# Norm squares added by accumulating DMA and VectorE, 1/rms inside the first product, memory scaled in the mixer's output stage

## The chip, the cores and the metric

The kernel runs on one core of a Trainium2 chip. The metric is the device time of one execution in microseconds (us). A "product" below is one matrix product of 24 matmuls into one PSUM bank.

## The reference

Two layers of a streaming-encoder block on 512 tokens of width 1024 (float32), and a final RMS norm:

```python
for l in range(2):
    x = x + 0.5 * swiglu(rmsnorm(x, ffn1_norm[l]), w1, w3, w2)          # hidden width 2816
    proj = rmsnorm(x, mix_norm[l]) @ w_in[l]                            # q, f, i, g | u
    o_a = hgrn2_mixer(q_a, f_a, i_a, g_a, ...)                          # gated linear recurrence, 4 heads
    o_b = multiscale_pool(u_b, pool_w[l], pool_scale[l])
    x = x + concatenate([o_a, o_b]) @ w_out[l]
    x = x + mem_cross_attention(rmsnorm(x, xa_norm[l]), rmsnorm(mem, mem_norm[l]), wq, wkv, wo)
    x = x + 0.5 * swiglu(rmsnorm(x, ffn2_norm[l]), w1, w3, w2)
return rmsnorm(x, final_norm)
# rmsnorm(x, g) = x * rsqrt(mean(x*x) + 1e-6) * g
```

## The kernel before

x is held transposed in SBUF (`xT`, eight tiles of 128 channels by 512 tokens). A float32 product is made of three float32r matmuls (`mm3`, lines 84 to 86): each operand is split into a rounded high part and a rest (`split`: ScalarE rounds, line 76 or 79; VectorE subtracts, line 77 or 80). Weights are split too, on the chip, after their load.

**Norms.** A `Norm` splits x times its gain as soon as a tile of x is final (`part`, giving `h`). 1/rms depends on the token alone, so it is multiplied in behind the product. `square` squares each tile on ScalarE, and GpSimd adds the eight squares one after another (line 388). `tick` is called behind each of the first products that use the norm: at tick `late` (2; 3 for the very first norm) the channels are summed by matmuls with ones and 1/rms is made (`col_rsqrt`), and a diagonal matrix of it (`diagonals`, eight small VectorE instructions); one tick later, that is behind the next product, a matmul spreads it to a row (`col_to_row`, ScalarE copies it as `rrow`). Only then can the first products be scaled and leave PSUM.

**FFN** (`ffn`). The hidden width is cut into 22 columns j in three parts. Columns 0 to 5 are plain: a product with w1, one with w3. The others go in pairs through `Pairs.block`, which makes seven half-size products in place of eight and needs the scaled right operands `b11` to `t4`. These are made by the generator `operands` in 14 steps, four in each column from j = 2. `project` multiplies by w2 in two halves and adds to x; in the second half it calls `after`, which is the next norm's `add`: for x tiles 0 to 3 behind its first two groups, for 4 to 7 behind each one's last matmul.

**Mixer, attention.** `mix` ends with `project` (groups of 24 matmuls, and after each an entry of `between`). `xattn` begins by loading `memT` in four pieces (`mt`), scaling them by 1/rms of the memory (line 914) and splitting them with the gain (`mn`); its first products, the keys, take `mn`. Its norm needs no row, and its 1/rms is not wanted before the scores.

**Weights** (`Weights`). `next` splits the next plain weights `SPLIT` = 3 ahead and loads up to `LOAD` = 7 ahead. Weights, split parts, `h`, operands and most other tiles share 38 slots of 4 KB.

**Order.** Each engine's queue is in the order of a scheduler that runs at build time: the program's order is its priority, and an instruction that its own time estimate finds not ready is passed over for a later one. On the chip the order is fixed.

Of the kernel before, what the change touches and what calls it, by code (L numbers as in the profile page):

```python
# [30 lines left out]

PLAIN = 6
PARTS = ((0, 8), (8, 16), (16, 22))
# [13 lines left out]
def trunk_kernel(ctx: ExitStack, tc: tile.TileContext, ap: dict, out: bass.AP):  # L47
# [41 lines left out]
    class Weights:  # L89

        SPLIT, LOAD = 3, 7

# [128 lines left out]
    for l in range(L):  # L223
        for w1, w3, w2 in (("ffn1_w1", "ffn1_w3", "ffn1_w2"), ("ffn2_w1", "ffn2_w3", "ffn2_w2")):
            for lo, hi in PARTS:
                for j in range(lo, hi):
                    if j < PLAIN:
                        wts.cols(ap[w1][l], j)
                        wts.cols(ap[w3][l], j)
                    elif j % 2 == 0:  # L230
                        wts.block(ap[w1][l], j)
                        wts.block(ap[w3][l], j)
                if hi == NJ and w1 == "ffn2_w1" and l == L - 1:
                    for k in [*range(lo, hi)] * 2:
                        wts.rows(ap[w2][l], k, 1, 0, D)
                else:
                    wts.project(ap[w2][l][lo * P:hi * P, :], hi - lo)
            if w1 == "ffn1_w1":
                for c in (4, 5, 6, 7, 0, 1, 2, 3, 12, 13, 14, 15):
# [12 lines left out]
                wts.project(ap["xa_wo"][l], NK)  # L252
# [87 lines left out]
    def diagonals(col, n=NT):  # L340

        dg = s_tile([P, 2, NT, P], F32R, "dg")
        hi = sm.tile([P, NT], F32R, tag="chi", name="chi")[:, :n]
        lo = sm.tile([P, NT], F32, tag="clo", name="clo")[:, :n]
        dve.tensor_copy(hi, col)
        dve.tensor_tensor(lo, col, hi.bitcast(F32), op=ALU.subtract)
# [12 lines left out]
    class Norm:  # L359
# [3 lines left out]

        def __init__(self, gain, l, row=True, late=2):
            self.gain, self.l, self.row, self.late = gain, l, row, late
            self.h = [None] * NK
            self.sq = None
            self.ticks = 0
            self.waiting = []
            self.r = self.col = None  # L370
# [250 lines left out]

    def ffn(norm, after, start=None, between=None):
        pairs = None
        for lo, hi in PARTS:
            a = []
            for j in range(lo, hi):
                if j >= PLAIN:
                    ahl = s_tile([P, 2, T], F32R, "ahl")
# [21 lines left out]
                norm.then(left)  # L650
                if j == 2:
                    pairs = Pairs(norm)
                    operands = pairs.operands()
                if j > 1:
                    next(operands, None)
                    next(operands, None)
                if p3 is None:
                    p3 = ps_tile()
                    col_matmul(p3, norm.h)
                norm.tick()  # L660
                t3 = tp.tile([P, T], F32, tag="up", name="t3", bufs=3)
# [8 lines left out]
                if between:  # L670
                    next(between, None)
                if j > 1:
                    next(operands, None)
                    next(operands, None)
            for _ in operands:
# [6 lines left out]

    def mix(l, norm, after):
        f = [s_tile([P, 2, T], F32, "f") for _ in range(2)]
# [6 lines left out]
        for h in range(H):  # L691
            ps = ps_tile()
            col_matmul(ps, norm.h)
            norm.tick()

# [18 lines left out]
        def products(a, b):  # L714

            t = tp.tile([P, T], F32, tag="sq", name="qk")
            hl = s_tile([P, 2, T], F32R, "qkp")
# [159 lines left out]
        def read(h):  # L877
# [4 lines left out]
            for i in range(NT):  # L882
# [3 lines left out]
                pe.matmul(ps[:, i * P:(i + 1) * P], vs[i], d0[:, i], start=False, stop=i == NT - 1)  # L886
            sq[h] = tp.tile([P, T], F32, tag="sq", name="osq")
            act.activation(sq[h], ps, AF.Square)
# [6 lines left out]
        def emit(h):  # L895
# [12 lines left out]
    def xattn(l, norm, after):  # L908

        mn = []  # L910
        for k2 in range(NK // 2):
            mt = s_tile([P, 2, M], F32, "mt")
            nc.sync.dma_start(mt, ap["memT"][:, 2 * k2:2 * k2 + 2])
            dve.tensor_tensor(mt, mt, memr.rearrange("p (o m) -> p o m", o=1).broadcast_to([P, 2, M]), op=ALU.mult)
            t = s_tile([P, 2, 2, M], F32R, "mn")
            for e in range(2):
                k = 2 * k2 + e
                split(t[:, 0, e], t[:, 1, e], mt[:, e], scale=vcol("mem_norm", l, k))
                mn.append((t[:, 0, e], t[:, 1, e]))
        kT = []  # L920
        for c in range(NK):
# [82 lines left out]
    def finish(a):  # L1004
# [12 lines left out]
        for half in range(2):  # L1017
# [4 lines left out]
            for js in [[j] for j in range(n - 2)] + tail:  # L1022
                for j in js:
                    w[j] = wts.next()
                for i in mine:
                    sl = slice(i * P, (i + 1) * P)
                    final = half and i == mine[1]
                    for hf in range(2):
# [7 lines left out]
                        dve.scalar_tensor_tensor(yi, accs[i, hf], 0.5, yi, op0=ALU.mult, op1=ALU.add)  # L1036
                        sq = tp.tile([P, 512], F32, tag="sq", name="fsq")
                        act.activation(sq, yi, AF.Square, accum_out=ss[:, i, hf:hf + 1])
# [20 lines left out]

    norm = Norm("ffn1_norm", 0, late=3)  # L1060
    wts.first()
    for d in range(NK):
        norm.part(d)
    for d in range(NK):
        norm.square(d)

    def begin(norm):
# [3 lines left out]
        for p, k2 in ((0, 0), (0, 1), (1, 0), (1, 1), (0, 2), (1, 2), (0, 3), (1, 3),  # L1071
# [16 lines left out]
    for l in range(L):  # L1088
        nxt = Norm("mix_norm", l)
        if l == 0:  # L1090
            ffn(norm, nxt.add, start=begin, between=early())
        else:
            ffn(norm, nxt.add)
        norm, nxt = nxt, Norm("xa_norm", l, row=False)
        mix(l, norm, nxt.add)
        norm, nxt = nxt, Norm("ffn2_norm", l)
        xattn(l, norm, nxt.add)
        norm = nxt
        if l + 1 < L:
            nxt = Norm("ffn1_norm", l + 1)  # L1100
            ffn(norm, nxt.add)
            norm = nxt
        else:
            finish(ffn(norm, None))

# [48 lines left out]
```

## Time and profile before

| | us |
|---|---|
| median of 3 runs (2178.58 to 2180.31) | 2178.6 |
| the profiled execution's own time | 2181.06 |
| its span, first to last instruction | 2179.3 |
| TensorE (PE) busy in the span | 2135.4 |
| VectorE (DVE) busy | 1403.0 |
| ScalarE (ACT) busy | 886.7 |
| GpSimd (POOL) busy | 289.8 |

The span is what the trace covers; the execution's own time has 1.8 us around it. PE busy 2135.4 of 2179.3 us leaves 43.9 us in which no matmul ran, 7.35 us of it ahead of the first one and 8.2 us behind the last. Where a matmul ran at a lower granted clock, it counts as busy all the same.

### The profile page before, as it was taken

Reading aid. Unit: us, or ns where it says so; the run is one execution under the profiler, and the core shown is the slowest. Engines: PE = TensorE matmul, PEld = TensorE weight load, DVE = VectorE, ACT = ScalarE, POOL = GpSimd, SP = SyncE. Lnnn points to the kernel's source line nnn. Section 1 sums busy time; section 2 is a strip of 40 time slices with the busy share of each in tenths; the row PEclk is TensorE's granted clock in tenths of the full one; section 3 lists DMA queues with packets and bytes.
Section 4 is the critical chain, followed back from the end, with each engine's and each line's share of the span. In section 5 each row is a group of like instructions: output and inputs, shape, how many; then the busy total and the mean of one; then the engine's idle time right before and its main releaser. Section 6 shows DMA issues by size and latency. Waiting matters only on the chain.

```text
span 2179.3 us, 31306 instructions
## 1 busy us (share of the span) xinstructions
PE 2135.4 (98%) x12470; PEld 1886.3 (87%) x12470; DVE 1403.0 (64%) x2212; ACT 886.7 (41%) x1372; POOL 289.8 (13%) x249
## 2 busy tenths in 40 slices
PE   7999999999999999999999999999999999999998
PEld 5789898788788888999988998988888888889896
DVE  5857566687736575756567575668775565757565
ACT  4535344312436243434444353453044443435254
POOL 2200002302200220000020000024211002100002
PEclk9999999999999999999999999999999999999999
DMA  5375453212323235645424646422023322465543
GB/s 204 93 191 138 141 147 135 67 59 87 107 97 122 78 90 157 172 134 155 144 72 120 175 130 179 150 83 87 31 97 116 116 89 75 117 181 138 162 126 110
DMA packets 103746, 265.55 MB, mean 122 GB/s; under 512 B 9904, under 2 KB 9904, under 8 KB 103600
## 3 DMA queue, kind: packets, MB, share of 16 engines
q1 hardware_dynamic: 93520, 228.37, 31.6%
q0 software_dynamic: 9216, 33.56, 9.0%
q8 instruction: 98, 1.61, 0.3%
q10 hardware_dynamic: 864, 1.63, 0.2%
q14 instruction: 48, 0.39, 0.1%
HBM read 261.42 MB, written 2.10 MB: 121 GB/s over the span
## 4 chain that ended last, share of the span: by engine, by line
PE 90%; DVE 5%; ACT 2%; issue 1%; POOL 1%; DMA 0%; SPq 0%; POOLq 0%; ACTq 0%; DVEq 0%
PE ps L86 17%; PE ps L84 17%; PE ps L85 17%; PE acc L84 11%; PE acc L85 11%; PE acc L86 11%; PE ps L765 2%; DVE wlo L77 1%; ACT whi L76 1%; DVE h L80 1%; PE ps L885 0%; POOL t L666 0%; DVE bsum L496 0%; DVE qkp L77 0%; PE ps L886 0%
## 5 line engine op out<-in xcount | busy, mean ns | idle before, releaser
L77 DVE TENSOR_TENSOR wlo<-raw,whi 128x1024 fp32r<-128x1024 f32 (+1 forms) x327 | 406.3, 1265 | 72.7 <-issue 44.8
L76 ACT CAST whi<-raw 128x1024 fp32r<-128x1024 f32 (+1 forms) x327 | 331.2, 1046 | 168.4 <-PE acc L86 65.9
L84 PE MATMUL ps<-h,whi 128*128 128x512 f32 x824 | 322.9, 393 | 8.8 <-ACT h L79 7.4
L85 PE MATMUL ps<-h,whi 128*128 128x512 f32 x824 | 321.5, 391 | 2.2 <-DVE h L80 2.2
L86 PE MATMUL ps<-h,wlo 128*128 128x512 f32 x824 | 321.0, 391 | 2.6 <-DVE wlo L77 2.6
L84 PE MATMUL acc<-bh,whi 128*128 128x256 f32 x768 | 218.2, 285 | 4.5 <-ACT whi L76 3.8
L84 PE MATMUL ps<-bh,whi 128*128 128x256 f32 x768 | 217.6, 284 | 1.2 <-ACT whi L76 1.2
L86 PE MATMUL ps<-bh,wlo 128*128 128x256 f32 x768 | 217.7, 284 | 0.5 <-DVE wlo L77 0.5
L85 PE MATMUL ps<-bl,whi 128*128 128x256 f32 x768 | 217.5, 283 | 0.0
L85 PE MATMUL acc<-bl,whi 128*128 128x256 f32 x768 | 217.4, 283 | 0.0
L86 PE MATMUL acc<-bh,wlo 128*128 128x256 f32 x768 | 217.1, 284 | 0.0
L77 DVE TENSOR_TENSOR wlo<-wsum,whi 128x1024 fp32r<-128x1024 f32 x128 | 156.6, 1224 | 77.1 <-ACT whi L76 42.0
L84 PEld LDWEIGHTS ps<-h,whi 128*128 128x128 f32 x824 | 155.2, 188 | 41.8 <-ACT h L79 7.4
L76 ACT CAST whi<-wsum 128x1024 fp32r<-128x1024 f32 x128 | 134.2, 1049 | 133.2 <-DVE wsum L164 106.2
L85 PEld LDWEIGHTS ps<-h,whi 128*128 128x128 f32 x824 | 155.2, 188 | 36.8 <-DVE h L80 5.4
L86 PEld LDWEIGHTS ps<-h,wlo 128*128 128x128 f32 x824 | 155.1, 188 | 36.7 <-DVE wlo L77 4.3
L134 POOL DMA_DIRECT2D wsum<-in_ffn_w_dram x64 | 55.6, 869 | 777.8 <-PE ps L86 260.2
L84 PEld LDWEIGHTS acc<-bh,whi 128*128 128x128 f32 x768 | 147.7, 192 | 6.6 <-ACT whi L76 4.9
L84 PEld LDWEIGHTS ps<-bh,whi 128*128 128x128 f32 x768 | 147.3, 192 | 2.5 <-ACT whi L76 1.8
L86 PEld LDWEIGHTS ps<-bh,wlo 128*128 128x128 f32 x768 | 147.6, 192 | 0.7 <-DVE wlo L77 0.7
L85 PEld LDWEIGHTS acc<-bl,whi 128*128 128x128 f32 x768 | 147.8, 192 | 0.5
L85 PEld LDWEIGHTS ps<-bl,whi 128*128 128x128 f32 x768 | 147.6, 192 | 0.6
(255 smaller groups left out, 4513.9 us busy)
## 6 DMA issues: line engine op xcount, KB each, us to landing
raw<-in_ffn_w_dram SPq DMA_DIRECT2D x205, 512.0 KB, 4.0
wsum<-in_ffn_w_dram SPq DMA_DIRECT2D x128, 256.0 KB, 3.1
wsum<-in_ffn_w_dram POOLq DMA_DIRECT2D x64, 512.0 KB, 5.6
raw<-in_ffn_w_dram SPq DMA_DIRECT2D x66, 256.0 KB, 4.9
raw<-in_w_in_dram SPq DMA_DIRECT2D x32, 512.0 KB, 3.3
raw<-in_w_out_dram SPq DMA_DIRECT2D x16, 512.0 KB, 3.4
raw<-in_xa_wk_dram SPq DMA_DIRECT2D x16, 512.0 KB, 3.3
raw<-in_xa_wq_dram SPq DMA_DIRECT2D x16, 512.0 KB, 3.3
```

The source lines that it names most:

```text
L76: act.copy(hi, src)
L77: dve.tensor_tensor(lo, src, hi.bitcast(F32), op=ALU.subtract)
L80: dve.scalar_tensor_tensor(lo, src, scale, hi.bitcast(F32), op0=ALU.mult, op1=ALU.subtract)
L84: pe.matmul(o, a[0], b[0], start=start, stop=False, skip_group_check=more)
L85: pe.matmul(o, a[0], b[1], start=False, stop=False, skip_group_check=more)
L86: pe.matmul(o, a[1], b[0], start=False, stop=stop, skip_group_check=more)
L134: nc.gpsimd.dma_start(s1, c2, accum_op=ALU.add)
L765: pe.matmul(o, kg[g][:, hh, sl], rhs, start=True, stop=True)
```

## The change

- `square`: of eight squares, the first goes to a tile `far`, the next three are added to it by accumulating DMAs from GpSimd's queue, and VectorE adds the other four and `far` (four additions). The very first norm has `far=0`: VectorE adds all (seven), and its squares are issued between the first products instead of ahead of them.
- `tick` is called four times within a product (`col_matmul`) in place of once behind it: 1/rms is made behind the fourth of eight k steps of the first product, and its row is made at that product's end (`rest` = 2). Attention's keys still call it once in three products.
- `operands` start as soon as the row is there, from j = 0, two steps behind each product. `diagonals` takes two wide instructions in place of eight small ones.
- Plain weights are split five ahead in place of three; the rules for blocks and for the end of the list stay.
- `memory` (loads, scaling and splitting of `mn`) is a generator of eight steps that the mixer's last `project` advances after its third to eighth group; two steps come behind it.
- PLAIN becomes a tuple of four sixes: no column changes its kind.

```diff
-        SPLIT, LOAD = 3, 7
+        SPLIT, LOAD = 5, 7
...
-            ahead = [*self.ahead(i, self.SPLIT + block)]
-            if i + self.SPLIT == len(self.src) - 1:
-                ahead.append(i + self.SPLIT)
+            ahead = [*self.ahead(i, 4 if block else self.SPLIT)]
+            if i + 3 == len(self.src) - 1:
+                ahead.append(i + 3)
...
     def diagonals(col, n=NT):
...
-        for i in range(n):
-            dve.tensor_scalar(dg[:, 0, i], ident, hi[:, i:i + 1].bitcast(F32), None, op0=ALU.mult)
-            dve.tensor_scalar(dg[:, 1, i], ident, lo[:, i:i + 1], None, op0=ALU.mult)
+        eye = ident.rearrange("p (o t) -> p o t", o=1).broadcast_to([P, n, P])
+        for c in range(2):
+            on = hl[:, c, :n].bitcast(F32).rearrange("p (n o) -> p n o", o=1).broadcast_to([P, n, P])
+            dve.tensor_tensor(dg[:, c, :n], eye, on, op=ALU.mult)
...
         def square(self, d):
-            s = tp.tile([P, T], F32, tag="sq", name="sq")
+            if self.n == 0 < self.FAR:
+                self.far = s = s_tile([P, T], F32, "far")
+            else:
+                s = tp.tile([P, T], F32, tag="sq", name="sq", bufs=4)
             act.activation(s, xT[d], AF.Square)
-            if self.sq is None:
+            if 0 < self.n < self.FAR:
+                nc.gpsimd.dma_start(self.far, s, accum_op=ALU.add)
+            elif self.n == self.FAR:
                 self.sq = s
-            else:
-                a = tp.tile([P, T], F32, tag="sqa", name="sqa")
-                pool.tensor_tensor(a, self.sq, s, op=ALU.add)
-                self.sq = a
+            elif self.n > self.FAR:
+                dve.tensor_tensor(self.sq, self.sq, s, op=ALU.add)
+                if self.far is not None and self.n == self.FAR + 1:
+                    dve.tensor_tensor(self.sq, self.sq, self.far, op=ALU.add)
+            self.n += 1
...
-            if self.ticks == self.late + 1 and self.row:
+            if self.ticks == self.late + self.rest and self.row:
...
-    def col_matmul(ps, parts, n=T):
+    def col_matmul(ps, parts, n=T, tick=None):
         whl = wts.next()
         for k in range(NK):
             mm3(ps[:, :n], (whl[0][:, k, :], whl[1][:, k, :]), parts[k], start=k == 0, stop=k == NK - 1)
+            if tick and k % 2:
+                tick()
...
+        def steps(n=-(-14 // (2 * plain - 2))):
+            nonlocal pairs, operands
+            if norm.r is None:
+                return
+            if pairs is None:
+                pairs = Pairs(norm)
+                operands = pairs.operands()
+            for _ in range(n):
+                next(operands, None)
...
-                    col_matmul(p1, norm.h)
-                norm.tick()
+                    col_matmul(p1, norm.h, tick=norm.tick)
...
-                if j == 2:
-                    pairs = Pairs(norm)
-                    operands = pairs.operands()
-                if j > 1:
-                    next(operands, None)
-                    next(operands, None)
+                steps()
...
         project(NK, parts, 1.0, after, order=MIX_OUT, tiles=(acc_tile, acc_tile),
-                between=[lambda: (scale(3), emit(2)), lambda: emit(3)])
+                between=[lambda: (scale(3), emit(2)), lambda: emit(3), *[lambda: next(mem, None)] * 8])
...
+    def memory(l, mn):
         for k2 in range(NK // 2):
             mt = s_tile([P, 2, M], F32, "mt")
             nc.sync.dma_start(mt, ap["memT"][:, 2 * k2:2 * k2 + 2])
+            yield
             dve.tensor_tensor(mt, mt, memr..., op=ALU.mult)
...
+            yield
...
-    norm = Norm("ffn1_norm", 0, late=3)
+    norm = Norm("ffn1_norm", 0, late=1, rest=1, far=0)
     wts.first()
     for d in range(NK):
         norm.part(d)
-    for d in range(NK):
-        norm.square(d)
...
     def begin(norm):
...
+            if norm.n < NK and p + k2 > 1:
+                norm.square(norm.n)
+            if p > 1 and k2 == 3:
+                norm.tick()
```

## Rows read from the trace of the kernel before

**Rows 1.** Page, busy us of an engine, its share of the span, its instructions.
```profile
PE 2135.4 (98%) x12470; PEld 1886.3 (87%) x12470; DVE 1403.0 (64%) x2212; ACT 886.7 (41%) x1372; POOL 289.8 (13%) x249
```

**Rows 2.** Waits of PE over the span: us in total, times, longest.
```profile
PE acc L333 <- POOL sqa L388: 9.8, 2, 4.9
PE ps L84 <- ACT h L79: 7.4, 1, 7.4
PE acc L84 <- ACT whi L76: 5.6, 6, 1.7
PE ps L86 <- DVE wlo L77: 3.9, 7, 1.0
PE ps L725 <- DVE atd L752: 2.6, 2, 1.3
PE ps L85 <- DVE h L80: 2.2, 3, 0.7
PE ps L84 <- DVE t L648: 1.4, 1, 1.4
```

**Rows 3.** Stretches: length, busy us (count) of PE, PEld, DVE, ACT, POOL; clock, DMA.
```profile
7.35:21.35 14.00, 10.75 (x29) 6.29 (x30) 13.21 (x12) 12.55 (x20) 11.15 (x7) 1.00 1.02 409
30.00:40.00 10.00, 10.00 (x49) 8.37 (x48) 1.01 (x7) 0.00 (x0) 1.03 (x1) 1.00 0.18 59
...
47.00:101.00 54.00, 49.77 (x242) 41.10 (x241) 47.10 (x64) 28.31 (x43) 13.38 (x9) 0.97 0.31 85
...
555.00:571.00 16.00, 16.00 (x72) 13.24 (x71) 9.96 (x9) 5.92 (x9) 4.79 (x3) 1.00 0.40 122
574.50:592.00 17.50, 12.22 (x73) 11.41 (x72) 14.04 (x22) 9.38 (x17) 6.64 (x5) 0.80 0.24 80
810.00:822.00 12.00, 10.81 (x87) 10.36 (x86) 10.80 (x16) 6.98 (x11) 1.59 (x1) 1.00 0.60 201
```

**Rows 4.** Timeline at layer 0's attention: start, us, engine, line, out<-in, idle before.
```profile
573.21 6.77 POOL L388 TENSOR_TENSOR sqa<-sqa,sq 128x512 f32<-128x512 f32 x4 [10.46 <-ACT sq L383]
...
578.78 1.75 DVE L914 TENSOR_TENSOR mt<-mt,memr 128x512 f32<-128x512 f32 x1
...
580.03 1.87 PE L333 MATMUL acc<-ones,sqa 128*128 128x1 f32 x8 [4.89 <-POOL sqa L388]
```

**Rows 5.** Groups of instructions: busy us, mean ns of one, idle before.
```profile
L388 POOL TENSOR_TENSOR sqa<-sqa,sq 128x512 f32<-128x512 f32 x48 | 80.5, 1677 | 83.5 <-ACT sq L383 80.7
...
L164 DVE TENSOR_TENSOR wsum<-wsum,raw 128x512 f32<-128x512 f32 x64 | 43.9, 685 | 0.7
```

**Rows 6.** Line 80: ns min/median/max of its instructions.
```profile
L80 DVE SCALAR_TENSOR_TENSOR h<-xall,vec,h x64: 737/1090/1795, 7.3 to 1815.0; 128x512 fp32r<-128x512 f32 x64
L80 DVE SCALAR_TENSOR_TENSOR mn<-mt,vec,mn x16: 477/482/485, 581.2 to 1658.0; 128x256 fp32r<-128x256 f32 x16
```

**Rows 7.** Line 134, accumulating DMAs of 512 KB: issue in ns, landing in us.
```profile
L134 POOL DMA_DIRECT2D wsum<-in_ffn_w_dram x64: 853/862/1037, 57.4 to 2086.8; - x64
...
DMA to landing us min/median/max: 5.2/5.6/10.3
```

**Rows 8.** Line 913, plain DMAs of 256 KB.
```profile
DMA to landing us min/median/max: 2.5/2.8/2.9
```

**Rows 9.** Timeline at ffn2 of layer 0: 1/rms, its row, the first operand.
```profile
754.94 0.16 DVE L335 TENSOR_SCALAR v<-acc 128x4 f32<-128x4 f32 x1 [4.54 <-PE acc L333]
...
757.89 0.28 DVE L349 TENSOR_SCALAR dg<-fixed,clo 128x128 fp32r<-128x128 f32 x1
...
763.06 0.59 ACT L400 COPY rrow<-acc 128x512 f32<-128x512 f32 x1 [14.73 <-PE acc L356]
...
771.97 0.74 DVE L472 SCALAR_TENSOR_TENSOR top<-xall,vec,rrow 128x512 f32<-128x512 f32 x1
```

**Rows 10.** Timeline at the end of ffn1, layer 0: the second and sixth square.
```profile
357.06 0.62 ACT L383 ACTIVATE sq<-xall 128x512 f32<-128x512 f32 x1
...
371.65 0.62 ACT L383 ACTIVATE sq<-xall 128x512 f32<-128x512 f32 x1
```

More of the change, by code (lines that the diff above doesn't have):

```diff
@@ L29 @@
 SLOTS = 38
-PLAIN = 6
+PLAIN = (6,6,6,6)
 PARTS = ((0, 8), (8, 16), (16, 22))
@@ L226, in trunk_kernel @@
                 for j in range(lo, hi):
-                    if j < PLAIN:
+                    if j < PLAIN[2 * l + (w1 == "ffn2_w1")]:
                         wts.cols(ap[w1][l], j)
@@ L342, in diagonals @@
         dg = s_tile([P, 2, NT, P], F32R, "dg")
[L343 to L346, printed above, removed]
-        for i in range(n):
-            dve.tensor_scalar(dg[:, 0, i], ident, hi[:, i:i + 1].bitcast(F32), None, op0=ALU.mult)
-            dve.tensor_scalar(dg[:, 1, i], ident, lo[:, i:i + 1], None, op0=ALU.mult)
+        hl = sm.tile([P, 2, NT], F32R, tag="chl", name="chl")
+        dve.tensor_copy(hl[:, 0, :n], col)
+        dve.tensor_tensor(hl[:, 1, :n], col, hl[:, 0, :n].bitcast(F32), op=ALU.subtract)
+        eye = ident.rearrange("p (o t) -> p o t", o=1).broadcast_to([P, n, P])
+        for c in range(2):
+            on = hl[:, c, :n].bitcast(F32).rearrange("p (n o) -> p n o", o=1).broadcast_to([P, n, P])
+            dve.tensor_tensor(dg[:, c, :n], eye, on, op=ALU.mult)
         return dg
@@ L359, in trunk_kernel, with __init__ @@
     class Norm:
-        def __init__(self, gain, l, row=True, late=2):
-            self.gain, self.l, self.row, self.late = gain, l, row, late
+        def __init__(self, gain, l, row=True, late=2, rest=2, far=4):
+            self.gain, self.l, self.row, self.late, self.rest, self.FAR = gain, l, row, late, rest, far
             self.h = [None] * NK
-            self.sq = None
+            self.sq = self.far = None
+            self.n = 0
             self.ticks = 0
@@ L619, in done, with ffn @@
             split(self.a[1][0], self.a[1][1], self.t[1])
-    def ffn(norm, after, start=None, between=None):
-        pairs = None
+    def ffn(norm, plain, after, start=None, between=None):
+        pairs = operands = None
+        def steps(n=-(-14 // (2 * plain - 2))):
[7 more added lines that the diff above has]
+                next(operands, None)
         for lo, hi in PARTS:
@@ L626, in ffn @@
             for j in range(lo, hi):
-                if j >= PLAIN:
+                if j >= plain:
                     ahl = s_tile([P, 2, T], F32R, "ahl")
@@ L650, in ffn @@
                 norm.then(left)
-                if j == 2:
-                    pairs = Pairs(norm)
-                    operands = pairs.operands()
-                if j > 1:
-                    next(operands, None)
-                    next(operands, None)
+                steps()
                 if p3 is None:
                     p3 = ps_tile()
-                    col_matmul(p3, norm.h)
-                norm.tick()
+                    col_matmul(p3, norm.h, tick=norm.tick)
                 t3 = tp.tile([P, T], F32, tag="up", name="t3", bufs=3)
@@ L671, in ffn @@
                     next(between, None)
-                if j > 1:
-                    next(operands, None)
-                    next(operands, None)
+                steps()
             for _ in operands:
@@ L680, in ffn, with mix @@
             project(hi - lo, a, 0.5, after if hi == NJ else (lambda d: None), tiles=(acc_tile, ps_tile))
-    def mix(l, norm, after):
+    def mix(l, norm, mem, after):
         f = [s_tile([P, 2, T], F32, "f") for _ in range(2)]
@@ L692, in mix @@
             ps = ps_tile()
-            col_matmul(ps, norm.h)
-            norm.tick()
+            col_matmul(ps, norm.h, tick=norm.tick)
             def forget(h=h, ps=ps):
@@ L714, in products @@
         def products(a, b):
-            t = tp.tile([P, T], F32, tag="sq", name="qk")
+            t = tp.tile([P, T], F32, tag="sq", name="qk", bufs=4)
             hl = s_tile([P, 2, T], F32R, "qkp")
@@ L886, in read @@
                 pe.matmul(ps[:, i * P:(i + 1) * P], vs[i], d0[:, i], start=False, stop=i == NT - 1)
-            sq[h] = tp.tile([P, T], F32, tag="sq", name="osq")
+            sq[h] = tp.tile([P, T], F32, tag="sq", name="osq", bufs=4)
             act.activation(sq[h], ps, AF.Square)
@@ L919, in xattn @@
                 mn.append((t[:, 0, e], t[:, 1, e]))
+            yield
+    def xattn(l, norm, mn, after):
         kT = []
@@ L1036, in finish @@
                         dve.scalar_tensor_tensor(yi, accs[i, hf], 0.5, yi, op0=ALU.mult, op1=ALU.add)
-                        sq = tp.tile([P, 512], F32, tag="sq", name="fsq")
+                        sq = tp.tile([P, 512], F32, tag="sq", name="fsq", bufs=4)
                         act.activation(sq, yi, AF.Square, accum_out=ss[:, i, hf:hf + 1])
@@ L1090, in trunk_kernel @@
         if l == 0:
-            ffn(norm, nxt.add, start=begin, between=early())
+            ffn(norm, PLAIN[0], nxt.add, start=begin, between=early())
         else:
-            ffn(norm, nxt.add)
+            ffn(norm, PLAIN[2], nxt.add)
         norm, nxt = nxt, Norm("xa_norm", l, row=False)
-        mix(l, norm, nxt.add)
+        mn = []
+        mem = memory(l, mn)
+        mix(l, norm, mem, nxt.add)
+        for _ in mem:
+            pass
         norm, nxt = nxt, Norm("ffn2_norm", l)
-        xattn(l, norm, nxt.add)
+        xattn(l, norm, mn, nxt.add)
         norm = nxt
@@ L1100, in trunk_kernel @@
             nxt = Norm("ffn1_norm", l + 1)
-            ffn(norm, nxt.add)
+            ffn(norm, PLAIN[1], nxt.add)
             norm = nxt
         else:
-            finish(ffn(norm, None))
+            finish(ffn(norm, PLAIN[3], None))
 def _layout(inputs):
```

2 lines of the change are left out of this document (removed).

## The prediction

> **What bounds the kernel now.** First the page's table of engines: TensorE is busy 2135.4 us of the 2179.3 us span [rows 1], so no other engine sets the time as a whole. The change takes no matmul away (PLAIN stays at six), so it can win only what TensorE idles, 43.9 us, and what a low clock costs; of the idle time 7.4 us are the wait for the first tile of x and some 8 us follow the last matmul, and neither is touched. Second, TensorE's list of waits [rows 2]: it names what is late. Third, windows around those waits [rows 3], which give the place: length less busy time is idle time, and the clock column shows where the matmuls that did run were slow. The reader should see five places:
> - the head, 7.35 to 21.35: 14.00 less 10.75, 3.25 us idle;
> - the wait for a PSUM bank that the row of 1/rms frees: 1.4 us, once (`t`, line 648);
> - the first FFN, 47 to 101: 4.23 us idle, and a mean clock of 0.97, which over 54 us is 1.6 us more; VectorE is busy 47.1 of the 54 us;
> - the start of attention, 574.5 to 592: 5.28 us idle and a clock of 0.80, up to 3.5 us more, so 8.8 us; the wait for `sqa` stands twice, so layer 1 has it too: 17.6 us;
> - the first block of the three later FFNs: 1.19 us each, 3.6 us; and the mixer's first level (`atd`), 1.3 us in each layer, 2.6 us [rows 2].
>
> All together 34.3 us, which is the most that the parts below can bring.
>
> **Attention's start.** TensorE runs dry after the mixer's product and waits 4.89 us until GpSimd has added the last squares (573.21 plus 6.77 is 579.98) [rows 4]. That addition is not what it needs: the keys take `mn`, and line 914 starts on the first piece of `mt` only at 578.78, behind the additions to x and the splits of `h`. The scheduler put the 1/rms matmuls into the hole. So the late work is the memory's. The change moves, per layer, four loads on SP's queue, four scalings on VectorE (1.75 us for the one shown, beside GpSimd), eight rounded parts on ScalarE and eight of 0.48 us on VectorE [rows 4, 6] into the output stage: at most 11 us of VectorE. In 16 us of that stage VectorE was busy 9.96 [rows 3], so 6 us are free in this stretch alone, which is three of the stage's eight groups (72 of 8 x 24 matmuls): hidden. The loads of 256 KB land in 2.8 us [rows 8] and are short of a group's 5.3 us. If that cover were gone, TensorE would wait as today. The last of four pieces has its scaling behind the end of the stage, so products start with six of eight k steps; I let each layer keep 1.8 us. Gain 2 x 7.0 = 14.0 us (bounds 2 x 5.3, the idle time alone without the two later pieces' wait growing, and 17.6).
>
> **Squares off GpSimd.** Removed: 56 GpSimd additions of about 1.68 us [rows 5]. Added: 35 VectorE additions (four for seven norms, seven for the first) at 0.69 us, the price of line 164, which also adds two float32 tiles in SBUF: 24 us; and 21 accumulating DMAs, 0.86 us of GpSimd each [rows 5, 7]. VectorE gets as much back: `h` took 1.09 us in the median and 1.80 at worst, but 0.74 at best [rows 6]; 64 of them at 0.35 us less are 22 us. So VectorE's total stays, and at a norm's end the four splits (about 1.4 us less together) pay for half of the four additions. In the head the same effect counts at once: three waits for `h` [rows 2] fall into a time when GpSimd adds for 11.15 of 14 us [rows 3], and the squares no longer stand between the `h` pieces on ScalarE. Gain 2.5 us of 3.25 (bounds 0, if the loads of x set the pace, and 3.25).
>
> **The accumulating DMAs' delay.** The trace has none within SBUF. From below, a plain 256 KB load lands in 2.8 us [rows 8]; from above, an accumulating one of 512 KB in 5.6 us in the median, 10.3 at worst [rows 7]. I take 4, between them for half the bytes. The three wait for each other. At the end of ffn1 the second square is done at 357.7 and the sixth, with which `far` is added, at 372.3 [rows 10]; `far` is complete at 369.7, or at 374.5 with 5.6 us each. So at 4 us it costs nothing, at 5.6 us VectorE waits about 2 us, still ahead of the matmuls on h[6]. SP's queue is not touched; GpSimd's holds nothing else there.
>
> One page speaks against this part. The issue of such a DMA took 0.85 to 1.04 us in all 64 cases, on a VectorE that is busy 64% of the time [rows 1, 7]. The Trainium skill, "SBUF — State Buffer", section "SBUF: two separate sides", warns that GpSimd cannot write descriptors while VectorE holds the shared port pair, so that such a DMA waits for the VectorE instruction. By that rule each of the 21 would be late by up to one VectorE instruction; by the row none was. What remains of it is in the third rival.
>
> **1/rms within the first product.** At ffn2 of layer 0 the column sums end at 754.94, the diagonals at 758.17, but the row is copied only at 763.06 and the first operand begins at 771.97 [rows 9]: 3.2 us are work, the rest is the program's order. After the change the row comes about two products (11 us) earlier, and the operands by 15 us or so. In the first FFN that moves VectorE work into a stretch where VectorE does 1.01 of 10 us [rows 3], and the 1.4 us wait for the bank goes. Of the 5.8 us in 47 to 101 I take 4.5 (bounds 2 and 5.8); of the later blocks' 3.6 I take 2.7, since operands no longer share VectorE and ScalarE with the first block's splits there (10.80 of 12 us busy) (bounds 0 and 3.6); of the mixer's 2.6 half, 1.3 (bounds 0 and 2.6). Splitting five ahead gives the plain products more margin in the same stretches and takes four more slots of 38; I count it into these terms. The new diagonals cost two instructions at 0.69 for eight that overlap within 1.7 us: nothing.
>
> The price: at the 1/rms matmuls TensorE now stands close behind the last square. In rows 4 the sums were complete 4.8 us after the last matmul of the stage; with VectorE's additions about 3.5. The fourth k step is done after 12 matmuls of 0.22 us, 2.7 us: 0.8 us too early. The row is planned for the product's end (6.4 us with the sums' own 0.95), and can be there after 3.5 + 0.95 + 3.2 + 0.3, 8.0: 1.6 us too early. The scheduler passes such matmuls over where its own estimate sees the delay, so each of six norms costs between 0 and 2.4 us. I take 0.7, as the waits of rows 2 that come from such near dependences average 0.6 to 0.9 (`wlo`, `whi`): 4.2 us.
>
> **Sum.** 14.0 + 2.5 + 1.4 + 4.5 + 2.7 + 1.3 = 26.4, less 4.2: 22 us. The profiled execution would go from 2181.1 to 2159 us; it lies 2.5 us above the median of the runs, so against 2178.6 I forecast **2156 us**.
>
> **Rivals.**
> - The norms' waits come at their full 2.4 us: six norms, 14.4 us instead of 4.2. For it: the order is fixed from estimates that did not see 20 us of waits in the trace before. Against it: other matmuls of the next product are ready. 2178.6 - 26.4 + 14.4 = 2167 us.
> - The memory's work does not come early: the build-time order may keep it behind the splits of `h`, as it did with loads that lay ready [rows 4]. Against it: the program now names it earlier. Without the 14.0 us: 2170 us. Both of these together give 2181, no change.
> - Slower: `far` is late. If the accumulations land in 10.3 us, as the slowest of 64 did, `far` is complete at 388.6, and VectorE, which works in order, holds the splits h[6] and h[7] behind it; TensorE has use for h[6] some 4 us into the product, so it stands about 12 us at each of the three norms behind an FFN, and about 5 us at the two behind attention, where the squares begin earlier: 46 us, 2178.6 - 22 + 46 = 2203 us. It decides from about 6 us per accumulation. Against it: half the bytes, and no HBM.
>
> **Chances.** The forecast 0.62 (own range 2144, all 34.3 us with no new wait, to 2165); the norms' waits 0.14; no early memory 0.09; both, 0.05; `far` late, 0.10. The range 2143 to 2173 leaves out the last two and little else. About 0.2% (4 us) is what a measurement of this kernel can tell from no change. Faster 0.85, same 0.05, slower 0.10.
>
> **What would show it.** In the profile after: no wait of 4.9 us and no lower clock at attention's start, with the first `mt` scaling ahead of the last additions to x; no line of GpSimd for `sqa`, and `h` at 0.75 us; the row of 1/rms some 9 us after a product begins; operands complete by j = 3 and no wait for `whi` at the first block. Wrong would make it: waits of TensorE at lines of the column sums or the diagonal's product, VectorE waiting for the DMA into `far`, or loads on SP's queue held back for slots at j = 2 to 4, where operands, `h` and deeper splits are held together.

## The result, and the profile after

The changed kernel takes 2151.8 us (median of 4 runs, 2149.14 to 2153.5), the kernel before 2179.5 beside it: a ratio of 0.9872, with an interval from 0.9855 to 0.9889. Forecast were 2156 us. In the profiled executions the span went from 2179.3 to 2147.4 us. TensorE idles 24.2 us of it, where it was 43.9, so 19.7 of the 31.9 us are idle time; the other 12.2 us are less busy time for the same matmuls. The mean granted clock went from 0.994 to 0.997, which is worth about 6.6 us of them (0.006 of 2179.3 less 0.003 of 2147.4, an estimate); what shortened the rest was not isolated.

The table of engines on the page of the kernel after (busy us, share, instructions) answers to [rows 1]:

```profile
PE 2123.2 (99%) x12470; PEld 1880.7 (88%) x12470; DVE 1381.4 (64%) x2161; ACT 885.3 (41%) x1372; POOL 226.5 (11%) x214
```

Its list of what TensorE waited for (us in total, times, longest; the five largest of nine) answers to [rows 2]:

```profile
PE ps L84 <- ACT h L79: 7.2, 1, 7.2
PE ps L86 <- DVE wlo L77: 2.5, 2, 2.1
PE acc L84 <- ACT whi L76: 1.7, 1, 1.7
PE ps L85 <- DVE h L80: 1.2, 2, 0.9
PE ps L84 <- DVE t L668: 0.9, 1, 0.9
```

The wait for `sqa` (9.8 us) is gone, and so are the mixer's for `atd` (2.6 us) and the ones for `whi` at the first blocks: the one that is left stands at the very end. No line of the column sums or of the row's product stands in the list. One wait is new, 2.1 us for a weight's rest (`wlo`).

Stretches of the kernel after (length, busy us and count of PE, PEld, DVE, ACT, POOL, clock, DMA share, GB/s): the head, the first FFN, the last part of the mixer's output stage, and attention's start. They answer to the windows of [rows 3].

```profile
7.20:21.20 14.00, 12.39 (x42) 8.41 (x43) 13.40 (x20) 14.00 (x22) 0.00 (x0) 1.00 1.03 407
...
42.00:96.00 54.00, 51.65 (x265) 43.99 (x264) 44.90 (x63) 27.78 (x42) 16.73 (x9) 0.97 0.38 114
542.00:567.20 25.20, 25.20 (x113) 20.87 (x112) 17.20 (x25) 13.06 (x21) 2.64 (x3) 1.00 0.52 136
567.20:584.00 16.80, 16.80 (x142) 16.76 (x141) 13.40 (x24) 10.27 (x18) 1.94 (x1) 1.00 0.50 161
```

Attention's start was 5.28 us idle at a mean clock of 0.80; now it is never idle, at full clock, and the same holds in layer 1. The first FFN is not better by much: 2.35 us idle where 4.23 were, and the clock of 0.97 is there again.

Why attention starts at once is in VectorE's timeline of the kernel after (start, us, line, out<-in):

```profile
542.97 0.68 DVE L925 TENSOR_TENSOR mt<-mt,memr 128x512 f32<-128x512 f32 x1
...
550.08 0.68 DVE L925 TENSOR_TENSOR mt<-mt,memr 128x512 f32<-128x512 f32 x1
...
556.25 0.68 DVE L925 TENSOR_TENSOR mt<-mt,memr 128x512 f32<-128x512 f32 x1
...
571.58 0.69 DVE L925 TENSOR_TENSOR mt<-mt,memr 128x512 f32<-128x512 f32 x1
```

and in TensorE's, the last matmul of the stage and the first of the keys:

```profile
567.12 0.39 PE L86 MATMUL acc<-h,wlo 128*128 128x512 f32 x1
567.35 0.28 PE L84 MATMUL ps<-mn,whi 128*128 128x256 f32 x1
```

Three of the four pieces of the memory are scaled inside the stage; the fourth comes 4.2 us after the keys' first matmul and still in time. In [rows 4] the first of them came at 578.78, when TensorE had already run dry.

The norm at ffn2 of layer 0, which answers to [rows 9], in the timeline of the kernel after, from the stage's first matmul:

```profile
726.27 0.39 PE L84 MATMUL ps<-h,whi 128*128 128x512 f32 x1
...
731.25 0.68 DVE L394 TENSOR_TENSOR sq<-sq 128x512 f32<-128x512 f32 x1
...
736.47 0.95 PE L333 MATMUL acc<-ones,sq 128*128 128x1 f32 x8
...
737.46 0.16 DVE L335 TENSOR_SCALAR v<-acc 128x4 f32<-128x4 f32 x1 [5.53 <-PE acc L333]
739.06 1.28 DVE L349 TENSOR_TENSOR dg<-fixed,chl 128x512 fp32r<-128x512 f32 x2
...
745.13 0.59 ACT L408 COPY rrow<-acc 128x512 f32<-128x512 f32 x1 [15.24 <-PE acc L356]
...
746.36 2.07 DVE L482 SCALAR_TENSOR_TENSOR top<-xall,vec,rrow 128x512 f32<-128x512 f32 x3
```

The squares are added up at 731.93, 5.7 us after the stage's first matmul (the prediction had about 3.5), so that the sums could not have run within the first product. The column sums run later still, at 736.47, and the row is copied 4.8 us after the diagonals are done, with ScalarE idle for 15.24 us ahead of it. Counted from the stage's first matmul (743.08 in the kernel before), the row's copy comes after 18.9 us where it came after 20.0 [rows 9], the first operand after 20.1 where it was 28.9. The program names this work within the first product; on the chip the sums come near the end of the second and the row later still, so the scheduler passed it over.

Last, what replaced GpSimd's additions, in the groups of the kernel after: issue of the accumulating DMAs in ns, their landing in us, and line 80 (to hold against [rows 6, 7]).

```profile
L390 POOL DMA_DIRECT2D far<-sq x21: 850/864/921, 355.7 to 1767.5; - x21
...
DMA to landing us min/median/max: 3.2/3.6/6.2
...
L80 DVE SCALAR_TENSOR_TENSOR h<-xall,vec,h x64: 739/743/753, 7.2 to 1784.2; 128x512 fp32r<-128x512 f32 x64
```

### The profile page after: what moved, and what is told of

Same layout as the page of the kernel before. It is cut to its first block, busy times and chain, and to the rows that moved or that the text cites. A ratio compares the mean times of both kernels' runs of the same rounds, so it can differ in the third digit from the quotient of the medians.

```text
span 2147.4 us, 31240 instructions
## 1 busy us (share of the span) xinstructions
PE 2123.2 (99%) x12470; PEld 1880.7 (88%) x12470; DVE 1381.4 (64%) x2161; ACT 885.3 (41%) x1372; POOL 226.5 (11%) x214
## 3 DMA queue, kind: packets, MB, share of 16 engines
q8 instruction: 98, 1.61, 0.3%
## 4 chain that ended last, share of the span: by engine, by line
PE 97%; DVE 1%; ACT 1%; issue 0%; POOL 0%; DMA 0%; SPq 0%; POOLq 0%; ACTq 0%; DVEq 0%
PE ps L84 19%; PE ps L86 19%; PE ps L85 19%; PE acc L84 12%; PE acc L85 12%; PE acc L86 12%; PE ps L776 2%; PE ps L896 0%; PE ps L803 0%; PE ps L897 0%; PE ps L880 0%; PE ps L999 0%; PE ps L333 0%; PE acc L333 0%; PE ps L736 0%
## 5 line engine op out<-in xcount | busy, mean ns | idle before, releaser
L77 DVE TENSOR_TENSOR wlo<-raw,whi 128x1024 fp32r<-128x1024 f32 (+1 forms) x327 | 400.6, 1246 | 69.8 <-ACT whi L76 61.8
L86 PEld LDWEIGHTS acc<-bh,wlo 128*128 128x128 f32 x768 | 147.3, 192 | 0.0
```

Of the source, the lines that this page charges most:

```text
L77: dve.tensor_tensor(lo, src, hi.bitcast(F32), op=ALU.subtract)
L86: pe.matmul(o, a[1], b[0], start=False, stop=stop, skip_group_check=more)
```

## The experiments

Twelve kernels ran: nine are the kernel after with one or more parts undone or altered, three are the kernel before with one or two parts alone. Ratios are to the kernel before on the same chip (medians 2179.5 to 2181.3 us), with their 95% interval. The runs of one kernel spread over 0.5 to 4.4 us, in a_pool_sq over 7.2 and in a_mem_back over 8.4, so differences of 2 to 4 us between two medians say little without a trace.

| kernel | median us | ratio |
|---|---|---|
| a_mem_back | 2167.7 | 0.9947 [0.9931, 0.9964] |
| b_memory | 2169.8 | 0.9947 [0.9931, 0.9964] |
| a_pool_sq | 2157.3 | 0.9900 [0.9884, 0.9917] |
| a_far0 | 2152.1 | 0.9870 [0.9854, 0.9885] |
| b_squares | 2177.8 | 0.9984 [0.9974, 0.9993] |
| a_split3 | 2200.7 | 1.0095 [1.0080, 1.0110] |
| a_tick_whole | 2149.0 | 0.9856 [0.9841, 0.9871] |
| a_whole_split3 | 2159.3 | 0.9901 [0.9886, 0.9916] |
| b_mem_split5 | 2150.6 | 0.9863 [0.9847, 0.9879] |
| a_ops_j2 | 2147.5 | 0.9847 [0.9832, 0.9861] |
| c_best | 2151.5 | 0.9863 [0.9848, 0.9878] |
| c_best2 | 2145.7 | 0.9842 [0.9824, 0.9859] |

### The memory's place

**a_mem_back** is the kernel after with the memory's work named behind the stage.

```diff
-                between=[lambda: (scale(3), emit(2)), lambda: emit(3), *[lambda: next(mem, None)] * 8])
+                between=[lambda: (scale(3), emit(2)), lambda: emit(3)])
```

> The changed kernel with the memory's scaling and splitting back at the start of attention. Theory M (the memory's lateness held attention's start; GpSimd's squares were only what stood in the hole): TensorE waits some 5 us again at each attention's start, at a lower clock, 14 to 17 us in all: 2166 to 2169 us. Rival S (the squares on GpSimd held it, and VectorE now adds them): under 1 us of wait, 2152 to 2155 us.

2167.7 us, 16 us more than the change. In its list TensorE waits for the memory, not for squares, once in each layer:

```profile
PE ps L84 <- ACT mn L79: 10.0, 2, 5.0
```

With the squares on VectorE and complete in time, the same 5 us are there. So the wait that the profile of before put down to `sqa` was the memory's, as the prediction read it.

**b_memory** is the kernel before with this part alone (the function `memory` of the change, advanced in `between`; 1/rms, squares and splits as before).

```diff
-                between=[lambda: (scale(3), emit(2)), lambda: emit(3)])
+                between=[lambda: (scale(3), emit(2)), lambda: emit(3), *[lambda: next(mem, None)] * 8])
```

> The kernel before with the memory's work in the mixer's output stage and nothing else. M: both waits of 4.9 us and the low clock go, 14 to 17 us: 2163 to 2167 us. S (GpSimd's squares hold attention's start): TensorE still waits for the sum, 2175 us or more.

2169.8 us, 11 us less than its own before (2181.0), and less gain than expected. Its list of TensorE's waits holds

```profile
PE ps L85 <- DVE mn L80: 4.3, 2, 2.1
```

a loss of 2.1 us in each layer, near the 1.8 us that the prediction allowed for the last piece. VectorE's timeline shows that it is the third piece, not the last: TensorE goes on at 580.43, when the first of these two lines is done, and only then is the last piece scaled.

```profile
578.90 1.48 DVE L80 SCALAR_TENSOR_TENSOR mn<-mt,vec,mn 128x256 fp32r<-128x256 f32 x1
580.30 0.68 DVE L914 TENSOR_TENSOR mt<-mt,memr 128x512 f32<-128x512 f32 x1
```

In the full change this wait is gone.

### The squares

**b_squares** is the kernel before with the squares alone: the new `square`, first norm `far=0`, nothing else.

```diff
-                a = tp.tile([P, T], F32, tag="sqa", name="sqa")
-                pool.tensor_tensor(a, self.sq, s, op=ALU.add)
...
+            if 0 < self.n < self.FAR:
+                nc.gpsimd.dma_start(self.far, s, accum_op=ALU.add)
...
+                dve.tensor_tensor(self.sq, self.sq, s, op=ALU.add)
```

> The kernel before with the squares by accumulating DMA and VectorE, nothing else. M: attention's start still waits, now for the memory's pieces, about 5 us in each layer; the head and some waits behind VectorE shrink: 2173 to 2178 us. S: the two waits of 4.9 us go with their low clock: 2168 us or less.

2177.8 us, 3.5 us less than before (2181.3). The wait at attention does not go, it changes its name:

```profile
PE ps L84 <- ACT mn L79: 9.9, 2, 5.0
```

**a_pool_sq** is the kernel after with the squares added one by one on GpSimd, as before.

```diff
-            elif self.n > self.FAR:
-                dve.tensor_tensor(self.sq, self.sq, s, op=ALU.add)
...
+            else:
+                a = tp.tile([P, T], F32, tag="sqa", name="sqa", bufs=2)
+                pool.tensor_tensor(a, self.sq, s, op=ALU.add)
```

> The changed kernel with the squares added one by one by GpSimd, as before. M: attention's start stays free of waits; what comes back is the slow h in the head and about 1 us here and there: 2153 to 2157 us. S: the waits for the sum of squares return, 10 us or more: over 2162 us.

2157.3 us: by medians the squares' part is worth 5.5 us within the change (the two intervals overlap), and without it there is no wait for `sqa` either, since the memory's work is early. Line 80 is slow again (median 1.09 us, 1.79 at worst).

**a_far0** lets VectorE add all eight squares at every norm, so that no DMA accumulates.

```diff
-        def __init__(self, gain, l, row=True, late=2, rest=2, far=4):
+        def __init__(self, gain, l, row=True, late=2, rest=2, far=0):
```

> The changed kernel with all eight squares of every norm added by VectorE, no accumulating DMA. Theory F (the DMAs are hidden and so would be three more additions of 0.69 us, in an output stage where VectorE waits for products): no change, 2149 to 2155 us. Rival (VectorE is what limits the norm's end, and the DMAs relieve it): 2156 us or more.

2152.1 us, the change's own time, and line 80 stays at 0.74 us. So what the squares' part brings comes from GpSimd's silence; that the DMA adds anything is not shown. It is not excluded either: the trace of a_far0 has 5.0 us of waits for `keep` where the change has 0.4, and makes them up at places where its granted clock stayed full.

### Five ahead, and the row within the first product

**a_split3** is the kernel after with plain weights split three ahead again.

```diff
-        SPLIT, LOAD = 5, 7
+        SPLIT, LOAD = 3, 7
```

> The changed kernel with plain weights split three ahead. Theory O (the earlier operands emptied VectorE and ScalarE ahead of the first block): no change over 2 us, 2150 to 2154 us, and no wait at the first block; perhaps less of the slot shortage in the first FFN. Rival D (the deeper split did it): the 1.2 us waits at the three first blocks and some of the first FFN's return, 2156 to 2160 us.

2200.7 us, 49 us more than the change and slower than the kernel before. Neither theory had this. TensorE's list:

```profile
PE ps L84 <- ACT whi L76: 20.2, 6, 5.6
PE ps L86 <- DVE wlo L77: 17.4, 5, 4.8
```

and ScalarE's, VectorE's and TensorE's timeline at ffn2 of layer 0, where the idle time before an instruction and what ended it stand in brackets:

```profile
743.07 1.03 ACT L76 CAST whi<-raw 128x1024 fp32r<-128x1024 f32 x1
758.44 0.58 ACT L408 COPY rrow<-acc 128x512 f32<-128x512 f32 x1 [14.34 <-PE acc L356]
758.92 1.05 ACT L76 CAST whi<-raw 128x1024 fp32r<-128x1024 f32 x1
...
763.51 1.98 DVE L77 TENSOR_TENSOR wlo<-raw,whi 128x1024 fp32r<-128x1024 f32 x1
765.55 0.79 PE L86 MATMUL ps<-h,wlo 128*128 128x512 f32 x1 [4.79 <-DVE wlo L77]
```

ScalarE stands idle for 14.34 us at the copy of the row, and the split of a weight, for which TensorE runs dry at 758.4, stands behind that copy. That order fits an estimate in which the row comes early (the estimate itself is in no trace); on the chip it comes behind two products, and the split, next in ScalarE's fixed order, comes after it. TensorE waits 1.62 us until 760.02 for the rounded part. It waits another 4.79 us, until 765.55, for the rest, which VectorE makes only from 763.51, behind four first operands (2.73 us) and two scaled products. In the 30 us from 742 its mean clock is 0.89.

**a_tick_whole** is the kernel after with `tick` once behind each product, as before (1/rms behind the second product, the row behind the third).

```diff
-        def __init__(self, gain, l, row=True, late=2, rest=2, far=4):
+        def __init__(self, gain, l, row=True, late=2, rest=1, far=4):
...
-            if tick and k % 2:
-                tick()
+        if tick:
+            tick()
```

> The changed kernel with one tick behind each whole product, so that the row of 1/rms comes behind the third. Theory P (the build-time order already held the 1/rms matmuls back behind two products, so the row came only some 2 us earlier than before): no change over 2 us, 2150 to 2154 us. Rival (an earlier row is what emptied the later stages): 4 to 6 us slower, 2156 to 2158 us.

2149.0 us, no worse than the change. At ffn2 of layer 0 the stage begins at 726.12 and the row is copied at 745.7, after 19.6 us, where the change has 18.9: naming it earlier moved it by 0.7 us.

**a_whole_split3** has both edits.

> The changed kernel with three ahead and one tick behind each whole product. Theory Q (with three ahead the slow-down came from the row's copy, which the early tick puts ahead of the weights' splits on ScalarE, where it waits some 14 us with the splits behind it): without the early tick the waits for whi and wlo go, 2149 to 2156 us. Rival (three ahead is too few for operands that start at j = 0): the waits stay, 2185 us or more.

2159.3 us: with the late tick, 41 of the 49 us are gone although splits are three ahead (10 us remain against a_tick_whole). ScalarE's timeline of this kernel, same norm:

```profile
734.64 2.94 ACT L76 CAST whi<-raw 128x1024 fp32r<-128x1024 f32 x3
751.60 0.59 ACT L408 COPY rrow<-acc 128x512 f32<-128x512 f32 x1 [14.02 <-PE acc L356]
```

Three weights are split ahead of the copy, where a_split3 had one. The copy holds up ScalarE for 14 us in both; what counts is what stands behind it. Of what remains, 4.1 us are one wait for `whi` in the first FFN, which a_split3 has too.

**b_mem_split5** is the kernel before with the memory's part and five ahead, nothing else: b_memory and

```diff
-        SPLIT, LOAD = 3, 7
+        SPLIT, LOAD = 5, 7
...
-            ahead = [*self.ahead(i, self.SPLIT + block)]
-            if i + self.SPLIT == len(self.src) - 1:
-                ahead.append(i + self.SPLIT)
+            ahead = [*self.ahead(i, 4 if block else self.SPLIT)]
+            if i + 3 == len(self.src) - 1:
+                ahead.append(i + 3)
```

> The kernel before with the memory's work in the output stage and plain weights split five ahead; squares, ticks and operands as before. Theory D' (the deeper split by itself takes away the waits at the three first blocks and most in the first FFN): 8 to 11 us less than the memory alone gave, 2159 to 2162 us. Rival (those waits need the earlier operands or the squares' change): 2166 us or more.

2150.6 us, some 8 us under the expected range, and the whole gain of the change. Splitting five ahead took 19 us off b_memory: 18.5 us of span (2168.3 to 2149.8), of which 11.0 are idle time (37.7 to 26.7 us) and 7.5 are less busy time for the same matmuls. The table of engines of b_memory, then of b_mem_split5:

```profile
PE 2130.6 (98%) x12470; PEld 1883.3 (87%) x12470; DVE 1402.1 (65%) x2212; ACT 886.8 (41%) x1372; POOL 288.1 (13%) x249
PE 2123.1 (99%) x12470; PEld 1880.8 (87%) x12470; DVE 1401.8 (65%) x2212; ACT 885.1 (41%) x1372; POOL 287.3 (13%) x249
```

In b_memory's list stood, beside the one for `mn`,

```profile
PE acc L84 <- ACT whi L76: 5.6, 6, 1.7
PE ps L725 <- DVE atd L752: 2.6, 2, 1.3
```

In the list of b_mem_split5 the waits for `mn` and `atd` are gone, and one for `whi` is left, at the very end:

```profile
PE ps L84 <- ACT keep L537: 3.9, 2, 3.6
PE ps L85 <- DVE h L80: 2.8, 5, 0.7
PE acc L84 <- ACT whi L76: 1.7, 1, 1.7
```

The first FFN, in the window of [rows 3], has neither idle time nor a lower clock:

```profile
47.00:101.00 54.00, 54.00 (x309) 47.72 (x308) 48.83 (x69) 30.76 (x47) 13.50 (x9) 1.00 0.35 93
```

The third piece of the memory is no earlier here: its rest ends 5.4 us after the first matmul of the keys (572.18), as in b_memory (575.02). But with more weights split ahead TensorE has about 45 matmuls of other keys to do until then, where b_memory had 26 and waited. Five ahead without the memory's part was not run.

### The operands' start

**a_ops_j2** lets the operands begin at column 2, as before, four steps per product.

```diff
-        def steps(n=-(-14 // (2 * plain - 2))):
+        def steps(j, n=-(-14 // (2 * plain - 4))):
...
-            if norm.r is None:
+            if norm.r is None or j < 2:
```

> The changed kernel with the operands' steps from j = 2, four in each column. Theory O: the waits of 1.2 us at the three first blocks and a part of the first FFN's return: 2155 to 2160 us. Rival (five ahead alone is enough there): no change, 2149 to 2154 us.

2147.5 us, 4 us less than the change by medians; the two intervals overlap, and the profiled executions differ by 2.2 us (spans of 2145.2 and 2147.4). The trace shows where that lies. The first FFN in the same window as the change's:

```profile
42.00:96.00 54.00, 54.00 (x303) 47.40 (x302) 48.89 (x68) 30.44 (x49) 15.37 (x9) 1.00 0.35 95
```

No idle time and full clock, where the change had 2.35 us and 0.97; 2.3 us of waits for `keep` (0.4 in the change) give a part back in the blocks behind it. So the change's one new wait comes with the early operands. Its weight was loaded late: the queue of SyncE (SP), which issues the plain loads, stood up to 20.7 us for a free slot there and issued the load at 52.71. ScalarE then split it at 55.68, and VectorE, with the operands' sums and rests in front, made its rest only from 59.37 to 60.59, just before TensorE goes on (60.64). The trace of c_best, below, tells the two apart.

### A better version

**c_best** is the kernel after with whole ticks (as in a_tick_whole), the 1/rms of the memory prepared six steps later, and the last copies of x out of PSUM shared between the engines:

```diff
-                act.copy(y[i][:, hf * 512:(hf + 1) * 512], ps)
+                (dve.tensor_copy if hf else act.copy)(y[i][:, hf * 512:(hf + 1) * 512], ps)
...
+        for _ in range(6):
+            yield
```

> A version meant to beat both: the changed kernel with one tick behind each whole product, the memory's 1/rms prepared only behind the first FFN's plain columns (two raw tiles less hold slots while its weights load), and the last eight copies of x shared between ScalarE and VectorE. If the slot shortage caused the 2.1 us wait for wlo at 60 us and ScalarE's copies the waits of 1.7 and 0.5 us at the end, with their low clock: 5 to 8 us less than the changed kernel, 2143 to 2147 us. If not, 2149 to 2152 us.

2151.5 us, no gain. The wait of 2.1 us in the first FFN stays, although the same weight is now loaded 5.5 us earlier:

```profile
47.23 0.33 SPq L142 DMA_DIRECT2D raw<-in_ffn_w_dram  x1
...
55.70 1.05 ACT L76 CAST whi<-raw 128x1024 fp32r<-128x1024 f32 x1
```

ScalarE splits it at 55.70 all the same (55.68 in the change), and VectorE makes its rest from 59.34 (59.37). So neither the late load nor the slots that the memory's first tiles hold set this wait; the operands that stand in front on ScalarE and VectorE do. Another wait stands at 286 us in the blocks; that the moved work causes it is not shown:

```profile
PE ps L84 <- ACT keep L547: 3.2, 2, 2.9
```

**c_best2** is the kernel after with the operands from column 2 (a_ops_j2), whole ticks, and the shared copies.

> A version meant to beat both, second try: the changed kernel with the operands' steps from j = 2, one tick behind each whole product, and the last eight copies of x shared between ScalarE and VectorE. The first gave 2147.5 us by itself, the copies take away some 2.5 us at the end: 2143 to 2147 us. Rival (each rearrangement moves some other wait by as much): 2147 to 2151 us.

2145.7 us (2143.74 to 2146.89): faster than both kernels, 0.9842 of the kernel before. The last 49.4 us of its span, and of the change's:

```profile
2092.30:2141.70 49.40, 39.32 (x193) 32.02 (x191) 30.03 (x41) 20.86 (x36) 13.20 (x10) 0.93 0.32 116
```

```profile
2098.00:2147.40 49.40, 37.75 (x171) 30.17 (x169) 24.95 (x33) 22.33 (x39) 12.82 (x10) 0.89 0.25 95
```

22 matmuls more fit into the same time, with VectorE taking half of the copies; a_ops_j2, without that, has 171 in its last 49.4 us as the change has. Against a_ops_j2 (2147.5) the 2 us of the medians are within the runs' spread.

## Why the prediction was right

The total was right, and its largest term for the reason given; several of the others were right in sum for a reason that the runs contradict, which is luck. The memory's part and five ahead alone reach the change's time (b_mem_split5, 2150.6 us). By medians the squares then bring 5.5 us within the change and the early operands take 4 away; what is left lies within the runs' spread.

- **Attention's start, 14.0 us.** Right: the memory's work was the late one, and it was hidden in the output stage. In the change all 17.6 us went (idle time and lower clock, both layers), because the 1.8 us kept for the last piece of each layer did not come. Alone (b_memory) it brings 11 us, with waits of 2.1 us for the third piece: the keys start with four of eight k steps, not six. Five splits ahead take this residue too, as TensorE then has other keys to start on (b_mem_split5).
- **Squares.** The sum on VectorE was about right: line 80 fell to 0.743 us in the median and 0.753 at worst, 64 times, which pays for the additions. VectorE's total fell by 21.6 us where it was to stay: line 80 took 26.2 us less and the additions of squares 23.9 more, as estimated, but the new diagonals, counted as nothing, took 9.6 less (27.6 to 18.0), and some 10 us lie spread over other lines. The head gained 1.6 us of the 2.5 taken (3.25 us idle, then 1.61). Alone the part is worth 3.5 us.
- **The accumulating DMAs' delay.** 3.6 us in the median for an estimate of 4, hidden as said. On the rule of the Trainium skill that stood against it ("SBUF — State Buffer", section "SBUF: two separate sides"): issue took 0.85 to 0.92 us in all 21 cases, so this trace shows no DMA of this kind whose issue was held up by VectorE. The section's warning is for VectorE instructions in a two-port performance mode, and whether any ran beside these DMAs the trace does not tell; the prediction applied it to every VectorE instruction. By a_far0's median the DMA brings nothing.
- **1/rms within the first product.** This step failed. The row was to come 11 us earlier, some 9 us after a product begins, and the operands 15; measured at ffn2 of layer 0 are 1.1 us (the row 18.9 us after) and 8.8 us. The squares were complete 5.7 us into the stage where 3.5 were taken, and the sums ran at 10.2. a_tick_whole, without the early tick, is no slower. The sentence that the scheduler passes such matmuls over stood in the prediction as a reason why the price would be small, and it is also why the gain is nil.
- **The norms' waits, 4.2 us.** None came, for the same reason: matmuls held back behind two products don't wait. The rival with 2.4 us each fails with it.
- **The first FFN, the blocks, the mixer's first level, 4.5 + 2.7 + 1.3 us.** The effects came (idle time in the first FFN 1.9 us less; the blocks' waits for `whi` 3.9 us less; `atd` 2.6 us less), but the cause was wrong, and that their sum (8.4 us) meets the 8.5 taken is luck: the first FFN kept its low clock and fell short, the blocks and the mixer gave more. They were credited to earlier operands, and the deeper split was to be a margin in the same terms. b_mem_split5 has no early operands and has these waits gone, and a_ops_j2 is faster than the change. The deeper split should have had a term of its own: 19 us on top of the memory's part.
- **What would make it wrong.** Of the three signs one came, loads held back for slots, at the 2.1 us in the first FFN; c_best shows that the held load is not what TensorE waits for there. a_ops_j2 takes that wait away.

By place, the traces give 17.6 (attention) + 1.6 (head) + 0.5 (`t`, 1.4 to 0.9) + 1.9 (first FFN) + 3.9 (blocks) + 2.6 (mixer) = 28.1 us of the 31.9 by which the profiled spans differ; the other 3.8 us are not placed. The medians differ by 27.7. The prediction had 26.4, less 4.2 for waits; of the gain that it fell short of, these 4.2 us are the larger part.

**Left open.** The wait for `keep` in the blocks, 0.4 us in the change, is 5.0 us in a_far0, 4.0 in a_pool_sq and 3.9 in b_mem_split5. In b_mem_split5 its longest (3.6 us) shows what stands in front of it on ScalarE:

```profile
160.01 1.04 ACT L76 CAST whi<-wsum 128x1024 fp32r<-128x1024 f32 x1 [6.58 <-issue]
160.97 0.64 ACT L537 COPY keep<-ps 128x256 f32<-128x256 f32 x2
```

The copy stands behind the split of a weight that is summed by accumulating DMAs (line 134), and such a DMA, issued at 149.13, landed just before 160.01. The 2.4 us in a_pool_sq look the same: issue at 794.25, split at 800.91, then the copy. Why these DMAs are late in one build and not in another stays open.

## What to carry to other kernels

Where engines work in a fixed order, how far ahead operands are prepared is a term of its own: here it decided whether an instruction that waits, such as a copy for a row that comes late, held up what TensorE needed next (five ahead in place of three was worth 10, 19 and 49 us in three settings). Naming work earlier in the program does not make it earlier if the scheduler passes it over, but it can put a wait ahead of other work in a queue; read the order on the engine, not in the source. And a wait is put down to one thing where several are late: without the squares on GpSimd the 5 us at attention's start came back under another name (b_squares), and they went only when the memory's work was moved.

## What the runs showed of the hardware

- An accumulating DMA of 256 KB within SBUF lands in 3.2 / 3.6 / 6.2 us (least, median, most of 21), against a median of 5.6 us for the 512 KB ones from DRAM of [rows 7].
- VectorE's instruction at line 80 took 0.74 to 0.75 us in all 64 cases once GpSimd's additions of squares were gone; with them it had a median of 1.09 and went up to 1.80 us [rows 6]. a_pool_sq, which puts them back into the change, has 1.09 and 1.79.
- What a short wait costs in clock differs from build to build. In six kernels TensorE waits 2.05 to 2.12 us for a weight's rest (`wlo`) at the same place of the first FFN. In the change and in a_tick_whole the granted clock then fell to the lower of its two levels (1.2 GHz), in the change for 3.4 us from 61.7; in a_mem_back, a_pool_sq, a_far0 and c_best it stayed at the higher one. The 5 us from 61 in the change, and in a_far0, where TensorE goes on at 61.12 after 2.11 us:

```profile
61.00:66.00 5.00, 5.00 (x16) 3.94 (x15) 5.00 (x8) 2.04 (x4) 4.04 (x1) 0.66 0.01 3
61.00:66.00 5.00, 4.88 (x21) 4.05 (x22) 5.00 (x8) 2.52 (x5) 3.56 (x1) 1.00 0.01 3
```
